# Gate and up products of the feed-forward blocks by Strassen's scheme, with the down product in three groups

## Chip, cores and metric

The kernel runs on one core of one Trainium2 chip. The metric is the device time of one execution in microseconds. In the text, TensorE is PE in the profile, its weight loads are PEld, VectorE is DVE, ScalarE is ACT, GpSimd is POOL and SyncE is SP. A "q" behind an engine's name (SPq, POOLq) means a DMA that this engine issues.

## The reference, cut to what matters

One inference step of a two-layer decoder for 512 prompt tokens and 32 sample tokens, which the kernel handles as one set of T = 544 tokens. Four times (two layers, two blocks each) a feed-forward block stands in it, of width 1024 and inner width 2816:

```python
D_MODEL, D_FF = 1024, 2816

def swiglu(x, w_gu, w_down):
    g, u = jnp.split(x @ w_gu, 2, axis=-1)
    return (jax.nn.silu(g) * u) @ w_down
...
    x = x + 0.5 * swiglu(rmsnorm(x, W['ffn1_norm'][i]), W['ffn1_w_gu'][i], W['ffn1_w_down'][i])
    # token mixer: recurrent block (layer 0) or differential attention (layer 1)
    x = x + 0.5 * swiglu(rmsnorm(x, W['ffn2_norm'][i]), W['ffn2_w_gu'][i], W['ffn2_w_down'][i])
    # a gated per-layer embedding; after layer 0 the shared keys and values are projected
```

Everything is float32 in the reference.

## The kernel before

Activations stand with channels on the 128 partitions and the 544 tokens along the free dimension: `x` is eight tiles (KC = 8) of 128 x 544. A product is worked out in three passes so that it keeps float32's accuracy on 32-bit "fp32r" operands: each operand is cut into a high part (a cast on ScalarE, `act.copy`) and a low part (source minus high part, a subtraction on VectorE), and high times high, high times low and low times high are summed in PSUM. So each block of 128 x 128 weights costs three matmuls for each half of the tokens. `split` (L205) does this for weights, `split_gain` (L217) for activations, with the norm's gain. The norm's other factor, one number per token, is the tile `rb`; it is applied behind the product, since it commutes with it. `mm3` (L188) issues the matmuls: for each input block k, three passes, each in two halves of 256 and 288 tokens.

Weights come in units of at most 128 x 1024 (512 KB). All steps of the program stand in one list, `steps`; the loop at its end keeps the loads (`load_unit`, on SP's queue, into three `raw` tiles) and the splits (`split_unit`, into three pairs `wh` and `wl`) a fixed number of units ahead of the step that runs. A `later` call puts a piece of work off by so many steps. The instructions are then ordered per engine by a scheduler, and every engine takes its own in that order, SP and GpSimd too.

In a feed-forward block (`ffn`), `gate(f)` and `up(f)` alternate for the 22 blocks f of 128 inner channels: one unit each, 48 matmuls each. The gate's result is multiplied by `rb` (L316) and goes through Silu (L317), the up result is multiplied by `rb` (L338) and by the gate's (L339), and the hidden block is split into `hh` (L340) and `hl` (L341), which hold all 22 blocks. Then `down(m, part)` forms eight output blocks m out of three parts of the 22 hidden blocks each (8, 7 and 7, the table `DOWN`), all three in one PSUM accumulation; L352 adds half of it to `x`, and `x_ready` makes the next stage's operands and the sum of squares for its norm. PSUM has four tiles of 128 x 1024 in turn (`new_ps`).

At the start, `x` and the first two weight units arrive in pieces in between, and gate and up of f = 0 run as the pieces come. Before the second block of layer 1, `x` can only be split into `xgh` and `xgl` once attention's output product has read them (`o_done`).

## Time and profile before

| quantity | value |
| --- | --- |
| device time, three runs | 2251.68, 2255.66 and 2256.83 us; median 2255.66 us |
| the profiled execution | 2249.68 us |
| its span, first to last instruction | 2247.8 us |
| mean granted TensorE clock | 0.992 of full speed |
| PE busy, PEld busy | 2194.9 us, 2139.6 us |
| DVE busy, ACT busy, POOL busy | 1069.4 us, 787.3 us, 187.7 us |
| matmuls | 17029 |

The profiled execution has 1.9 us outside its span and lies 6.0 us (0.27%) under the median of the three runs. Matmuls are pipelined, so a matmul's own duration in a row is longer than its share of the time; the spacing of matmuls is read from a stretch of time and the number of them in it.

### The profile page before, as it was taken

To read this page: it belongs to the slowest core of one execution; us is meant where nothing else is said; L and a number is where in the kernel's file an instruction comes from. 1 tells how busy PE (TensorE), PEld (TensorE's weight loads), DVE (VectorE), ACT (ScalarE), POOL (GpSimd) and SP (SyncE) were. 2 spreads that over 40 slices of the span, in tenths; PEclk is the share of its full clock that TensorE was granted. 3 is DMA by queue.
4 is the path that set the end of the run, shared out by engine and by line. 5 is a ranking of instruction groups with operands and counts; after the bars stand their busy time and mean duration, and the time that the engine had idled before them with its cause. 6 is when DMAs were issued, how large, how long until landed. Compare 5 with 4: busy or idle time off the path is not lost.

```text
span 2247.8 us, 39360 instructions
## 1 busy us (share of the span) xinstructions
PE 2194.9 (98%) x17029; PEld 2139.6 (95%) x17029; DVE 1069.4 (48%) x1661; ACT 787.3 (35%) x1132; POOL 187.7 (8%) x219
## 2 busy tenths in 40 slices
PE   9999999999999999999999999999879999999997
PEld 9999999999999999999899999999646999999997
DVE  7444423676544442357444444226656544443255
ACT  4222222596322222244232222223654422222243
POOL 0000001121000000011000000012430200000003
PEclk9999999999999999999999999999989999999998
DMA  4222233255222223233742322347992322223331
GB/s 160 92 85 88 87 88 88 96 125 132 85 87 93 85 87 90 81 100 114 230 154 85 94 86 82 111 129 214 243 279 63 113 86 90 89 84 86 90 108 51
DMA packets 87901, 248.89 MB, mean 111 GB/s; under 512 B 11120, under 2 KB 23168, under 8 KB 87600
## 3 DMA queue, kind: packets, MB, share of 16 engines
q1 hardware_dynamic: 78640, 217.13, 32.0%
q0 software_dynamic: 8400, 28.66, 4.8%
q8 instruction: 133, 2.18, 0.4%
q10 hardware_dynamic: 688, 0.60, 0.1%
q14 instruction: 40, 0.33, 0.1%
HBM read 216.18 MB, written 17.58 MB: 104 GB/s over the span
## 4 chain that ended last, share of the span: by engine, by line
PE 90%; ACT 2%; DMA 2%; DVE 2%; issue 1%; POOL 1%; another core or an unknown queue 0%; SPq 0%; DVEq 0%; POOLq 0%; ACTq 0%
PE ps L197 82%; PE ps L760 2%; PE g L197 1%; DMA raw<-in_wq 1%; PE s L197 1%; DMA vt<-vscr 0%; PE o L1162 0%; DMA xgh<-in_cache_k,idx 0%; PE ss L1178 0%; DMA x<-in_cache_v,idx 0%; PE S L989 0%; PE s L1109 0%; DMA x<-in_x 0%; ACT L447 0%
## 5 line engine op out<-in xcount | busy, mean ns | idle before, releaser
L206 ACT CAST wh<-raw 128x1024 fp32r<-128x1024 f32 (+2 forms) x334 | 336.1, 1007 | 1165.9 <-PE ps L197 1033.5
L197 PE MATMUL ps<-xgh,wl 128*128 128x256 f32 (+1 forms) x3360 | 697.0, 288 | 2.1 <-DMA wl<-raw 2.1
L197 PE MATMUL ps<-xgh,wh 128*128 128x256 f32 (+1 forms) x3360 | 695.9, 289 | 2.5 <-DVE x L1293 1.1
L197 PE MATMUL ps<-xgl,wh 128*128 128x256 f32 (+1 forms) x3360 | 694.3, 288 | 0.1
L197 PEld LDWEIGHTS ps<-xgh,wh 128*128 128x128 f32 x3360 | 543.5, 189 | 4.3 <-DVE x L1293 1.3
L197 PEld LDWEIGHTS ps<-xgl,wh 128*128 128x128 f32 x3360 | 541.6, 189 | 0.3 <-DVE xgl L219 0.3
L197 PEld LDWEIGHTS ps<-xgh,wl 128*128 128x128 f32 x3360 | 538.3, 188 | 2.5 <-DMA wl<-raw 2.5
L207 DVE TENSOR_TENSOR wl<-raw,wh 128x1024 fp32r<-128x1024 f32 (+2 forms) x334 | 389.4, 1166 | 289.9 <-ACT wh L206 285.3
L197 PE MATMUL ps<-hh,wl 128*128 128x256 f32 (+1 forms) x1408 | 290.9, 288 | 0.0
L197 PE MATMUL ps<-hh,wh 128*128 128x256 f32 (+1 forms) x1408 | 290.5, 287 | 0.0
L197 PE MATMUL ps<-hl,wh 128*128 128x256 f32 (+1 forms) x1408 | 288.3, 286 | 0.0
L197 PEld LDWEIGHTS ps<-hl,wh 128*128 128x128 f32 x1408 | 225.7, 188 | 0.0
L197 PEld LDWEIGHTS ps<-hh,wh 128*128 128x128 f32 x1408 | 225.0, 188 | 0.0
L197 PEld LDWEIGHTS ps<-hh,wl 128*128 128x128 f32 x1408 | 224.3, 188 | 0.0
L338 DVE TENSOR_TENSOR t<-ps,rb 128x544 f32<-128x544 f32 x88 | 63.7, 724 | 325.8 <-PE ps L197 325.8
L265 POOL TENSOR_TENSOR acc<-acc,sq 128x544 f32<-128x544 f32 x42 | 68.0, 1620 | 1671.1 <-ACT sq L264 1671.0
L316 DVE TENSOR_TENSOR t<-ps,rb 128x544 f32<-128x544 f32 x88 | 63.8, 724 | 213.5 <-PE ps L197 213.5
L340 ACT CAST hh<-t 128x544 fp32r<-128x544 f32 x88 | 57.0, 648 | 73.3 <-DVE t L339 73.3
L352 DVE SCALAR_TENSOR_TENSOR x<-ps,x 128x544 f32<-128x544 f32 x32 | 23.2, 725 | 109.8 <-PE ps L197 109.8
L339 DVE TENSOR_TENSOR t<-t,t 128x544 f32<-128x544 f32 x88 | 63.8, 725 | 10.0 <-ACT t L317 1.5
L341 DVE TENSOR_TENSOR hl<-t,hh 128x544 fp32r<-128x544 f32 x88 | 63.3, 719 | 5.1 <-ACT hh L340 5.1
L317 ACT ACTIVATE t<-t 128x544 f32<-128x544 f32 x88 | 58.0, 660 | 7.3 <-DVE t L316 6.7
(369 smaller groups left out, 2094.2 us busy)
## 6 DMA issues: line engine op xcount, KB each, us to landing
raw<-in_ffn_gu SPq DMA_DIRECT2D x174, 512.0 KB
raw<-in_ffn_dn SPq DMA_DIRECT2D x64, 448.0 KB
raw<-in_ffn_dn SPq DMA_DIRECT2D x32, 512.0 KB
raw<-in_rg_in SPq DMA_DIRECT2D x16, 512.0 KB
raw<-in_ple_gate SPq DMA_DIRECT2D x16, 512.0 KB
kst<-kscr SPq DMA_DIRECT2D x16, 512.0 KB
wl<-raw POOLq DMA_DIRECT2D x15, 512.0 KB, 4.7
raw<-in_rg_out SPq DMA_DIRECT2D x8, 512.0 KB
```

What stands on the lines that cost most here:

```text
L197: pe.matmul(ps[:, p0:p1], w[:, wc * P : (wc + 1) * P], a[:, k, t0:t1], start=first and q == 0 and s == 0, stop=last and q == n - 1 and s == 2,
L206: first = act.copy(hi, src)
L207: eng.tensor_tensor(lo, src, hi.bitcast(F32), op=OP.subtract)
L265: (eng or (dve if m == KC - 1 else pool)).tensor_tensor(norm["acc"], norm["acc"], sq, op=OP.add)
L316: dve.tensor_tensor(t1, body(ps), norm["rb"], op=OP.mult)
L317: act.activation(t1, t1, AF.Silu)
L338: dve.tensor_tensor(t2, body(ps), norm["rb"], op=OP.mult)
L339: dve.tensor_tensor(t2, t2, t1, op=OP.mult)
L340: act.copy(box["hh"][:, f, :], t2)
L341: later(lambda: dve.tensor_tensor(box["hl"][:, f, :], t2, box["hh"][:, f, :].bitcast(F32), op=OP.subtract))
L352: dve.scalar_tensor_tensor(x[:, m, :], body(ps), 0.5, x[:, m, :], op0=OP.mult, op1=OP.add)
L760: pe.matmul(banks[c], a[:, k, t0:t1], w[:, wv], start=k == 0 and s == 0, stop=k == KC - 1 and s == 2)
```

## The change

The gate's and the up product's weights for one f are seen as a matrix of two by two blocks: the first and second half of the 1024 input channels (four blocks of 128 each), times gate and up. The tokens are cut into two halves of TH = 272. Two outputs (gate, up) for two halves of tokens out of two halves of channels are eight block products; Strassen's scheme (in Winograd's form) forms them from seven products of sums and differences, each 4 x 3 matmuls of 128 x 272.

The activations' sums and differences are formed once per block of the program (`operand_main`, `operand_more`; the new pair of tiles `e`). The weights' sums are formed for every f. Of seven weight operands of 128 x 512, three are stored weights (the unit x, with two of them, and the tile `a`), two are formed by a load followed by an accumulating DMA from GpSimd's queue into the tile `r` (two buffers), and two by additions on VectorE (`sum6`, `sum3`), which need `r` and x. So each f has three units: x, y (first half of `r`) and z (second half of `r`), and `a`, which `low4` splits on its own into the single-buffered `w4h`, `w4l`. The seven products run as steps s0 to s6, with two of them (s1, s4) one f behind: s0(f), s1(f-1), s2(f), s3(f), s4(f-1), s5(f), s6(f). Products 7, 4, 6 and 3 go on in a PSUM area in which an earlier product's partial sum has just been copied out (L453, L468, L501) or read (L460, L479). `first_cycle` does f = 0, product by product interleaved over k.

`rb` is applied to the gate only; the up result stays without it, and the down product gets it instead (`down_done`). The 22 hidden blocks are formed in the three groups of `DOWN`: after 8 (7, 7) of them come all eight down products of this group, each added to `x`. `hh` and `hl` hold eight blocks, used again by each group.

```diff
@@ -287,82 +301,313 @@
...
+    def operand_main(m, gain):
+        xm = x[:, m, :]
+        if m < KC // 2:
+            u = (F.get("w") or F["tmp"]).tile([P, T], F32, tag="t2", name="u", bufs=2 if F.get("w") else 1)
+            act.copy(u[:, :TH], xm[:, :TH])
+            dve.tensor_tensor(u[:, TH:], xm[:, :TH], xm[:, TH:], op=OP.subtract)
+            xm = u
...
+    def operand_more(m, gain):
+        k = m - KC // 2
+        pp = F.get("w") or F["tmp"]
+        bk = pp.tile([P, T], F32, tag="t1", name="bk")
+        bm = pp.tile([P, T], F32, tag="t1", name="bm")
+        e = pp.tile([P, 3, TH], F32, tag="cc", name="e", bufs=2 if F.get("w") else 1)
+        act.activation(bk, x[:, k, :], AF.Copy, scale=v(gain, k))
+        act.activation(bm, x[:, m, :], AF.Copy, scale=v(gain, m))
+        dve.tensor_tensor(e[:, 0], bm[:, TH:], bk[:, TH:], op=OP.subtract)
+        dve.scalar_tensor_tensor(e[:, 1], e[:, 0], -1.0, bk[:, :TH], op0=OP.mult, op1=OP.subtract)
+        dve.scalar_tensor_tensor(e[:, 2], e[:, 1], -1.0, bm[:, :TH], op0=OP.mult, op1=OP.subtract)
+        split(F["e"][0][:, k], F["e"][1][:, k], e)
...
+    def second(q, k):
+        if q in (1, 5):
+            return [t.parts[0][:, k, TH * (q == 5) : TH * (q == 5) + TH] for t in (xgh, xgl)]
+        if q in (2, 3):
+            return [t.parts[1][:, k, TH * (q == 3) : TH * (q == 3) + TH] for t in (xgh, xgl)]
+        return [t[:, k, {7: 0, 6: 1, 4: 2}[q], :] for t in F["e"]]
...
+    def product(ps, q, w, c0, ks=range(KC // 2), first=True):
+        wh, wl = w
+        for k in ks:
+            bh, bl = second(q, k)
+            for s, (a, b) in enumerate(((wh, bh), (wh, bl), (wl, bh))):
+                pe.matmul(
+                    ps, a[:, c0 + k * P : c0 + k * P + P], b,
+                    start=first and k == 0 and s == 0, stop=k == KC // 2 - 1 and s == 2, skip_group_check=True,
+                )
...
+        def late_low(hi, lo, src):
+            act.copy(hi, src)
+            later(lambda: dve.tensor_tensor(lo, src, hi.bitcast(F32), op=OP.subtract))
...
+        def unit_y(f):
+            src = wgu[l, f]
+            u = U[f]
+            def load():
+                r = u["r"] = F["w"].tile([P, 4, 512], F32, tag="r", name="r")
+                sp.dma_start(r[:, 0:4:2, :], src[:, 1:3, :])
+                pool.dma_start(r[:, 0:4:2, :], src[:, 0:2, :], accum_op=OP.add)
+                u["a"] = F["w"].tile([P, 512], F32, tag="a", name="a")
+                sp.dma_start(u["a"], src[:, 0, :])
+            def cut():
+                sum6(f)
+                hi, lo = pair()
+                late_low(hi, lo, u["r"][:, 0:2, :].rearrange("p k n -> p (k n)"))
+                return hi, lo
+            return {"load": load, "split": cut, "open": lambda: F.get("w") is not None}
...
+        def unit_z(f):
+            u = U[f]
+            def cut():
+                sum3(f)
+                hi, lo = pair()
+                late_low(hi, lo, u["r"][:, 2:4, :].rearrange("p k n -> p (k n)"))
+                return hi, lo
+            return {"load": lambda: None, "split": cut, "open": lambda: True}
+        def sum6(f):
+            u = U[f]
+            if "s6" not in u:
+                u["s6"] = dve.tensor_tensor(u["r"][:, 1, :], u["r"][:, 0, :], u["x"][:, :512], op=OP.add)
+        def sum3(f):
+            u = U[f]
+            if "s3" not in u:
+                u["s3"] = dve.tensor_tensor(u["r"][:, 3, :], u["r"][:, 1, :], u["x"][:, 512:], op=OP.add)
...
+        def low4(f):
+            u = U[f]
+            u["w4"] = [F["w"].tile([P, 512], F32R, tag=n, name=n, bufs=1) for n in ("w4h", "w4l")]
+            late_low(*u["w4"], u["a"])
...
+        def begin(f):
+            u = U[f]
+            u["ps"] = new_ps()
+            u["b"], u["a_"] = u["ps"][:, :TH], u["ps"][:, 512 : 512 + TH]
+            u["cc"] = F["w"].tile([P, 3, TH], F32, tag="cc", name="cc")
+        def s0(f):
+            u = U[f]
+            begin(f)
+            product(u["b"], 1, ready[u["ix"]], 0)
+            act.copy(u["cc"][:, 0], u["b"])
+        def s1(f):
+            u = U[f]
+            product(u["b"], 7, ready[u["iz"]], 0, first=False)
+            t1 = u["t1"] = F["w"].tile([P, T], F32, tag="t1", name="t1")
+            dve.tensor_tensor(t1[:, TH:], u["b"], u["cc"][:, 2], op=OP.add)
+            dve.tensor_tensor(t1[:, TH:], t1[:, TH:], norm["rb"][:, TH:], op=OP.mult)
+            finish()
...
+        def s2(f):
+            u = U[f]
+            u["c"] = new_ps()[:, :TH]
+            product(u["c"], 5, ready[u["iy"]], 0)
+            act.copy(u["cc"][:, 2], u["c"])
...
+        def s3(f):
+            u = U[f]
+            product(u["a_"], 2, ready[u["ix"]], 512)
+            up_first(f)
+            finish()
...
+        def s4(f):
+            u = U[f]
+            product(u["b"], 4, u["w4"], 0, first=False)
+            t1 = u["t1"]
+            dve.tensor_tensor(t1[:, :TH], u["b"], norm["rb"][:, :TH], op=OP.mult)
+            act.activation(t1, t1, AF.Silu, scale=-1.0)
+            def hidden():
+                t2, q = u["t2"], f - H["a"]
+                dve.tensor_tensor(t2, t2, t1, op=OP.mult)
+                act.copy(H["hh"][:, q, :], t2)
+                later(lambda: dve.tensor_tensor(H["hl"][:, q, :], t2, H["hh"][:, q, :].bitcast(F32), op=OP.subtract), 3 if f < H["b"] - 1 else 1)
+            later(hidden, 2 if f < H["b"] - 1 else 1)
+        def s5(f):
+            u = U[f]
+            if f + 1 < H["b"]:
+                sum6(f + 1)
+            product(u["b"], 6, ready[u["iy"]], 512, first=False)
+            act.copy(u["cc"][:, 1], u["b"])
+            finish()
+        def s6(f):
+            u = U[f]
+            product(u["c"], 3, ready[u["iz"]], 512, first=False)
+            dve.tensor_tensor(u["t2"][:, TH:], u["c"], u["cc"][:, 1], op=OP.add)
+            low4(f)
...
+        def first_cycle(f):
+            u = U[f]
+            begin(f)
+            u["c"] = new_ps()[:, :TH]
+            for k in range(KC // 2):
+                product(u["b"], 1, ready[u["ix"]], 0, [k])
+                product(u["c"], 5, ready[u["iy"]], 0, [k])
+            act.copy(u["cc"][:, 0], u["b"])
+            act.copy(u["cc"][:, 2], u["c"])
+            for k in range(KC // 2):
+                product(u["a_"], 2, ready[u["ix"]], 512, [k])
+                product(u["c"], 3, ready[u["iz"]], 512, [k], first=False)
+                product(u["b"], 6, ready[u["iy"]], 512, [k], first=False)
+            up_first(f)
+            finish()
+            act.copy(u["cc"][:, 1], u["b"])
+            finish()
+            dve.tensor_tensor(u["t2"][:, TH:], u["c"], u["cc"][:, 1], op=OP.add)
+            low4(f)
+            norm_done()
...
+        def down_done(m, part):
+            ps = H.pop(("ps", m))
+            t = F["w"].tile([P, T], F32, tag="t1", name="dn")
+            dve.scalar_tensor_tensor(t, body(ps), 0.5, norm["rb"], op0=OP.mult, op1=OP.mult)
+            dve.tensor_tensor(x[:, m, :], x[:, m, :], t, op=OP.add)
+            if part == len(DOWN) - 1:
...
+        def step(fn, *args):
+            add(None, lambda: fn(*args), -1)
+        for part, (a, b) in enumerate(DOWN):
+            for f in range(a, b):
+                u = U[f]
+                u["ix"], u["iy"], u["iz"] = (add_unit(q(f)) for q in (unit_x, unit_y, unit_z))
+                if f == a:
+                    add(None, lambda a=a, b=b: group(a, b))
+                if f == 0:
+                    step(first_cycle, 0)
+                    continue
+                step(s0, f)
+                if f > a:
+                    step(s1, f - 1)
+                step(s2, f)
+                step(s3, f)
...
+                    step(s4, f - 1)
+                step(s5, f)
+                step(s6, f)
+            step(s1, b - 1)
+            add(wdn[l, 0][:, a:b, :], down(0, part))
+            step(s4, b - 1)
+            step(down_rest, part)
+            for m in range(1, KC):
                 add(wdn[l, m][:, a:b, :], down(m, part))
...
         def o_done(m, ps):
...
             if m == KC - 1:
                 for k in range(KC):
-                    split_gain(xgh[:, k, :], xgl[:, k, :], x[:, k, :], v(gain_out, k))
+                    operand_main(k, gain_out)
+            if m >= KC // 2:
+                operand_more(m, gain_out)
...
+    def may_load():
+        if at["dma"] >= n:
+            return False
+        u = units[at["dma"]]
+        if isinstance(u, dict):
+            return at["dma"] < at["split"] + 6 and u["open"]()
+        return at["dma"] < at["split"] + 3
+    def pump(hold):
+        while at["split"] < min(n, at["done"] + 3 - max(hold, 0)):
+            while at["dma"] <= at["split"]:
+                load_unit()
+            split_unit()
+        while may_load():
+            load_unit()
...
+    def quarters(w):
+        r = w.reshape(2, 2, KC // 2, P, 2, FC, P).transpose(0, 5, 3, 4, 1, 2, 6)
+        return np.ascontiguousarray(np.stack([r[:, :, :, 0, 1], r[:, :, :, 0, 0], r[:, :, :, 1, 0], r[:, :, :, 1, 1]], 3)).reshape(2, FC, P, 4, 512)
```

Also changed: pools move so that the tiles `e`, `r`, `a` and the new temporaries fit, `tables()` is issued after the fifth down product of the first group, and the loads of units x, y, z may run up to six units ahead of the splits.

The order in which VectorE takes its work in a feed-forward block, before, for one f. Names are those of the code, with a number for each allocation (`ps`: a PSUM tile; `hl_198`: the low hidden part):

```order
L316 TENSOR_TENSOR t1_945<-ps_896,rb_367 128x544
L207 TENSOR_TENSOR wl_949<-raw_775,wh_948 128x1024
L338 TENSOR_TENSOR t2_1003<-ps_954,rb_367 128x544
L339 TENSOR_TENSOR t2_1003<-t2_1003,t1_945 128x544
L207 TENSOR_TENSOR wl_1008<-raw_834,wh_1007 128x1024
L341 TENSOR_TENSOR hl_198<-t2_1003,hh_197 128x544
```

These are four passes over 544 tokens and two weight splits.

And now, for one f in the middle of a group, from the last row of the f ahead. `r_2035` and `raw_2001` are the tile `r` and the unit x of f + 1, `r_1912` is the tile `r` of f itself, with the rows between in the order of their steps:

```order
L492 TENSOR_TENSOR hl_247<-t2_1996,hh_246 128x544
L427 TENSOR_TENSOR r_2035<-r_2035,raw_2001 128x512
L432 TENSOR_TENSOR r_2035<-r_2035,raw_2001 128x512
L460 TENSOR_TENSOR t1_2213<-ps_2060,cc_2061 128x272
L461 TENSOR_TENSOR t1_2213<-t1_2213,rb_348 128x272
L371 TENSOR_TENSOR wl_2218<-r_1912,wh_2217 128x1024
L479 TENSOR_TENSOR t2_2248<-ps_2186,cc_2187 128x272
L371 TENSOR_TENSOR wl_2251<-raw_2001,wh_2250 128x1024
L485 TENSOR_TENSOR t1_2213<-ps_2060,rb_348 128x272
L371 TENSOR_TENSOR w4l_2309<-a_1915,w4h_2308 128x512
L490 TENSOR_TENSOR t2_2122<-t2_2122,t1_2213 128x544
L371 TENSOR_TENSOR wl_2285<-r_2035,wh_2284 128x1024
```

VectorE's two sums in the newly arrived `r_2035` now stand ahead of the partial gate (L460, L461) and ahead of the last use of the other buffer, `r_1912` (the row `wl_2218`). SP's queue in the same place:

```order
L382 DMA raw_2127<-in_ffn1_gu 128x1024
L403 DMA a_1915<-in_ffn1_gu 128x512
L400 DMA r_2035<-in_ffn1_gu 128x2x512
L382 DMA raw_2253<-in_ffn1_gu 128x1024
L403 DMA a_2038<-in_ffn1_gu 128x512
L400 DMA r_2161<-in_ffn1_gu 128x2x512
```

The load into a buffer `r` is followed on GpSimd's queue by its accumulation, `r_1912`, `r_2035`, `r_2161` in turn, one after each load. `r_2161` takes the buffer of `r_1912`, so its load waits for the row `wl_2218` above; the sums of `r_2161` then stand one cycle later in VectorE's queue, again ahead of the row that frees `r_2035`.

At the program's start VectorE's queue now holds these rows (`e`, `el`: the new activation operand; `acc`: sum of squares; `r_254` and `r_261`: the `r` of f = 1 and f = 2; `wl_371`: the unit x of f = 1):

```order
L221 TENSOR_TENSOR el_103<-e_193,eh_102 128x816
L334 TENSOR_TENSOR e_209<-bm_208,bk_207 128x272
L279 TENSOR_TENSOR acc_217<-acc_217,sq_237 128x544
L335 SCALAR_TENSOR_TENSOR e_209<-e_209,bk_207 128x272
L371 TENSOR_TENSOR w4l_337<-a_118,w4h_336 128x512
L336 SCALAR_TENSOR_TENSOR e_209<-e_209,bm_208 128x272
L221 TENSOR_TENSOR accl_340<-acc_217,acch_339 128x544
L432 TENSOR_TENSOR r_254<-r_254,raw_252 128x512
L221 TENSOR_TENSOR el_103<-e_209,eh_102 128x816
L427 TENSOR_TENSOR r_261<-r_261,raw_259 128x512
L432 TENSOR_TENSOR r_261<-r_261,raw_259 128x512
L479 TENSOR_TENSOR t2_332<-ps_267,cc_268 128x272
```

They stand behind 39 others, among them eight splits of `x` and three of weights. The sums for f = 2 (`r_261`, in the buffer that f = 0 frees) stand ahead of the split of f = 1's own unit x.

## Rows read from the trace of the kernel before

**Rows 1.** Page: busy time by engine, chain by engine, chain by line.

```profile
PE 2194.9 (98%) x17029; PEld 2139.6 (95%) x17029; DVE 1069.4 (48%) x1661; ACT 787.3 (35%) x1132; POOL 187.7 (8%) x219
PE 90%; ACT 2%; DMA 2%; DVE 2%; issue 1%; POOL 1%; another core or an unknown queue 0%; SPq 0%; DVEq 0%; POOLq 0%; ACTq 0%
PE ps L197 82%; PE ps L760 2%; PE g L197 1%; DMA raw<-in_wq 1%; PE s L197 1%; DMA vt<-vscr 0%; PE o L1162 0%; DMA xgh<-in_cache_k,idx 0%; PE ss L1178 0%; DMA x<-in_cache_v,idx 0%; PE S L989 0%; PE s L1109 0%; DMA x<-in_x 0%; ACT L447 0%
```

**Rows 2.** Windows by stage: gate/up, down, key projection, second layer's second gate/up start, program start.

```profile
core 0: us, PE busy (x) PEld busy (x) DVE busy (x) ACT busy (x) POOL busy (x), PEclk, DMA share, GB/s
50.00:230.00 180.00, 180.00 (x1436) 180.00 (x1435) 79.47 (x103) 50.70 (x61) 0.00 (x0) 1.00 0.28 89
275.00:406.00 131.00, 131.00 (x1053) 131.00 (x1052) 39.44 (x41) 33.19 (x39) 9.53 (x6) 1.00 0.31 89
1038.00:1082.00 44.00, 43.90 (x350) 43.82 (x351) 31.08 (x55) 12.08 (x15) 3.13 (x6) 1.00 0.50 152
1742.00:1779.00 37.00, 37.00 (x295) 37.00 (x296) 17.71 (x21) 18.44 (x25) 11.49 (x8) 1.00 0.46 128
0.00:30.00 30.00, 27.38 (x190) 26.50 (x191) 20.58 (x35) 18.50 (x27) 2.66 (x9) 1.00 0.69 226
```

**Rows 3.** Timeline of VectorE, 150 to 158 us: start, duration, operation, idle before it.

```profile
154.52 0.73 DVE L338 TENSOR_TENSOR t<-ps,rb 128x544 f32<-128x544 f32 x1 [3.92 <-PE ps L197]
155.35 0.73 DVE L339 TENSOR_TENSOR t<-t,t 128x544 f32<-128x544 f32 x1
155.99 1.22 DVE L207 TENSOR_TENSOR wl<-raw,wh 128x1024 fp32r<-128x1024 f32 x1
157.12 0.72 DVE L341 TENSOR_TENSOR hl<-t,hh 128x544 fp32r<-128x544 f32 x1
```

**Rows 4.** Groups by form: ScalarE casts and Silu.

```profile
L206 ACT CAST wh<-raw 128x1024 fp32r<-128x1024 f32 x256 | 269.2, 1052 | 875.6 <-PE ps L197 744.8 <-issue 104.1 <-PE ps L760 12.6
L317 ACT ACTIVATE t<-t 128x544 f32<-128x544 f32 x88 | 58.0, 660 | 7.3 <-DVE t L316 6.7 <-DVE e_g L1396 0.5
```

**Rows 5.** A weight load: VectorE row, load's issue, windows of the transfer.

```profile
599.15 1.22 DVE L207 TENSOR_TENSOR wl<-raw,wh 128x1024 fp32r<-128x1024 f32 x1
...
600.40 0.33 SPq L168 DMA_DIRECT2D raw<-in_ffn_gu  x1
...
600.50:601.00 0.50, 0.50 (x7) 0.50 (x6) 0.50 (x1) 0.00 (x0) 0.00 (x0) 1.00 0.00 0
601.00:601.50 0.50, 0.50 (x7) 0.50 (x6) 0.00 (x1) 0.00 (x0) 0.00 (x0) 1.00 0.75 66
603.00:603.50 0.50, 0.50 (x6) 0.50 (x5) 0.00 (x0) 0.01 (x1) 0.00 (x0) 1.00 0.55 221
603.50:604.00 0.50, 0.50 (x6) 0.50 (x5) 0.30 (x1) 0.50 (x1) 0.00 (x0) 1.00 0.00 0
```

**Rows 6.** Timelines of SP and ScalarE: loads of in_wv, and the cast that waits.

```profile
1087.01 0.92 SPq L168 DMA_DIRECT2D raw<-in_wv  x2
...
1091.11 1.05 ACT L206 CAST wh<-raw 128x1024 fp32r<-128x1024 f32 x1 [4.27 <-DMA raw<-in_wv]
```

**Rows 7.** Accumulating transfer: ScalarE row, GpSimd's issue, page's landing times.

```profile
480.09 1.04 ACT L213 ACTIVATE wl<-wh 128x1024 fp32r<-128x1024 f32 x1
...
481.43 0.85 POOL L214 DMA_DIRECT2D wl<-raw  x1 [3.87 <-ACT wl L213]
...
wl<-raw POOLq DMA_DIRECT2D x15, 512.0 KB, 4.7
...
qst<-sph POOLq DMA_DIRECT2D x32, 64.0 KB, 5.7
```

**Rows 8.** Chain in order of time: start and length of pieces.

```profile
9.95 16.36 PE ps L197 x128
27.65 385.09 PE ps L197 x3072
...
1741.92 36.44 PE ps L197 x288
```

More of the change, by code (lines that the diff above doesn't have):

```diff
@@ L141, in trunk_kernel, with add_unit @@
     steps = []
+    units, keeps, raw, ready = [], [], {}, {}
+    def add_unit(unit, keep=None):
+        units.append(unit)
+        keeps.append(keep)
+        return len(units) - 1
     def add(unit, fn, hold=0, keep=None):
+        if unit is not None:
+            add_unit(unit, keep)
         steps.append((unit, fn, hold, keep))
@@ L172, in split_unit @@
     def split_unit():
+        u = units[at["split"]]
+        if isinstance(u, dict):
+            ready[at["split"]] = u["split"]()
+            at["split"] += 1
+            return
         t, cols = raw.pop(at["split"])
@@ L178, in split_unit @@
             lo = wp.tile([P, 1024], F32R, tag="wl", name="wl")
-        with ExitStack() as order:
-            if at["split"] == 5:
-                order.enter_context(tc.issue_after(norm["read"].ins))
-            done_by[at["split"]] = (split_adding if at["split"] in slow else split)(h[:, :cols], lo[:, :cols], t[:, :cols])
+        done_by[at["split"]] = (split_adding if at["split"] in slow else split)(h[:, :cols], lo[:, :cols], t[:, :cols])
         ready[at["split"]] = h, lo
@@ new lines, in operand @@
+    def operand(m, gain, pp=None):
+        F["tmp"] = pp
+        operand_main(m, gain)
+        if m >= KC // 2:
+            operand_more(m, gain)
+    def second(q, k):
[13 more added lines that the diff above has]
+                )
@@ new lines, in go, with down_rest, group @@
+                down_part(m, part, range(a, b), w, True, True)
+                down_done(m, part)
+                if beside and part == 0 and m == 4:
+                    beside()
+            return go
+        def down_rest(part):
+            a, b = DOWN[part]
+            down_part(0, part, range(a + 4, b - 1), H["w0"], False, False)
+        def group(a, b):
+            H["a"], H["b"] = a, b
+            if a == 0:
+                hp, H["close"] = open_pool("ffnh", bufs=1, side="right")
+                H["hh"] = hp.tile([P, KC, T], F32R, name="hh")
+                H["hl"] = hp.tile([P, KC, T], F32R, name="hl")
@@ L524, in out_step @@
             return go
-        base = len([u for u, _, _, _ in steps if u is not None]) + 2 * KC
+        base = len(units) + 2 * KC
         slow.update(range(base - 8, base + 2))
@@ L1272, in early_more @@
                 mm3(*A["w", m], [(k, k) for k in range(4, 7)], xgh, xgl, first=False, last=False)
-        base = len([u for u, _, _, _ in steps if u is not None]) + KC
+        base = len(units) + KC
         slow.update(range(base + 0, base + 6))
@@ L1431, in trunk_kernel @@
     add(None, start)
-    ffn(0, "ffn1", "mix0", late=True)
-    steps.insert(6, (None, begin_tables, 0, None))
+    ffn(0, "ffn1", "mix0", beside=begin_tables)
     recurrent("ffn20")
@@ L1441, in trunk_kernel @@
     ple_final(1)
[L1444 to L1445 removed]
     n = len(units)
+    def may_load():
+        if at["dma"] >= n:
+            return False
+        u = units[at["dma"]]
+        if isinstance(u, dict):
+            return at["dma"] < at["split"] + 6 and u["open"]()
[4 more added lines that the diff above has]
+                load_unit()
+            split_unit()
+        while may_load():
+            load_unit()
     for u, fn, hold, _ in steps:
```

211 lines of the change are left out of this document (110 added, 101 removed).

## The prediction

> **What bounds the kernel now.** First the page: TensorE is busy for 2194.9 us, 98% of the span, with weight loads beside it for 2139.6 us, and in the chain of work that ended last it has 90%, of which the matmuls of `mm3` (L197) alone are 82% [rows 1]. No other engine reaches half. Then the windows by stage: in 50 to 230 us (gate and up) TensorE never idles and issues 1436 matmuls in 180 us, so one costs 125.3 ns; VectorE is busy for 79.47 us of the 180, ScalarE for 50.70, the DMA engines for 28% [rows 2]. The down products look the same (1053 matmuls in 131 us, VectorE 39.44). So fewer gate and up matmuls is time saved, one for one, as long as the others deliver; the question is what becomes late.
>
> **Matmuls removed.** Per f there were 2 units x 48 = 96 matmuls, now 7 x 12 = 84. The mean width was (256 + 288)/2 = 272 and stays 272, so I keep 125.3 ns. Over 22 x 4 = 88 f that is 88 x 12 x 0.1253 = **-132.3 us**; a cycle of one f falls from 12.03 to 10.53 us. Down matmuls stay as many.
>
> **What VectorE, ScalarE and the DMA have per f.** VectorE's rows start 0.64 us apart at 544 columns (155.35 to 155.99) and 1.13 us apart at 1024 (155.99 to 157.12); a row that needs the one ahead of it adds 0.19 (154.52 to 155.35 is 0.83) [rows 3]. That is 1.02 ns a column and 0.085 us an instruction: 0.61 at 512, 0.36 at 272. Per f it now has three splits of 1024 (3.39), a split and two sums of 512 (1.83), five rows of 272 (1.80) and two of 544 (1.28), 8.3 us, and with two or three dependent pairs 8.7 of the 10.53; it had 79.47/180 x 12.03 = 5.3 of 12.03. ScalarE: three casts at 1.052 us and a Silu at 0.66 [rows 4], and by width half a cast (0.53), three copies of 272 (about 0.35 each) and a cast of 544 (0.65): 6.1 us. DMA: 0.28 of 12.03 us for 1 MB before is 3.4 us; now 1.75 MB, with 0.5 MB of sums read back and written once more 2.25 MB, is at most 7.6. None passes 10.53, so in a steady cycle TensorE stays the bound, if every operand arrives in turn.
>
> **The ring of two `r`.** This is what may not. A new `r` is loaded when the z split of the f two ahead has read its buffer; the load lands, GpSimd issues the accumulation, it lands, and only then can VectorE take the two sums. In its queue these stand, as the order shows, ahead of the partial gate of f (L460, L461) and of f's z split, which frees the other buffer and so starts the next such trip. One trip is thus a cycle of its own, and if it takes longer than 10.53 us TensorE waits: product 4 goes on in the PSUM area that L460 reads, and L460 is queued behind the sums.
>
> The legs of a trip. (a) SP wakes in about 0.05 us (600.37 to 600.40), and the transfer's data end in the slice 603.00 to 603.50, some 3.1 us after the split that freed the buffer [rows 5]; a queue in which ScalarE waits for a load gives 4.1 (1087.01 to 1091.11) [rows 6]. Both carry 512 KB, as here. I take the middle, 3.6. (b) GpSimd issues 0.3 us after what it waits for (481.13 to 481.43), and an accumulation of 512 KB lands 4.7 us after its issue [rows 7]; one of 64 KB, in another stage, needs 5.7. I take 4.7. With a wake on either side that makes L = 8.7 us; the bounds are 8.2 (3.1 us) and 10.2 (4.1 and 5.7). (c) VectorE: the two sums, dependent (0.80 + 0.61), L460 (0.55, behind them), L461 (0.36) and the z split (1.22, to its end): 3.5 us. A trip is 12.2 us and the excess over a cycle e = 1.67 us (1.17 to 3.17).
>
> It does not bind in every f. At each group's start two `r` have been fetched beside the down products, which use none, and the group's first cycle has only five products. Of a group's seven or eight cycles I count four as bound, and 0.3 us of slack left over. There are 12 groups (three in each of four blocks): 12 x (4 x 1.67 - 0.3) = **+76.6 us**; at the bounds 53 and 148. It is hidden altogether if L is 7.0 or less.
>
> **The program's start.** Before, the chain has 128 matmuls in the 16.36 us from 9.95, and from 27.65 us they run without a gap for 385 us [rows 8]. Of the 190 matmuls in the first 30 us [rows 2], 18 fall behind 27.65, 24 only warm the engine up and 4 are the norm's: 144 products' matmuls are done by then. Now f = 0 has 60 matmuls, and f = 1 cannot begin until VectorE has split its unit x. VectorE stands ahead of it with four subtractions and eight splits of x, twelve rows and four 816-wide splits for `e`, weight splits, sums and squares, about 28 us by the column price, from the 5th microsecond: 34. Next in its queue are the sums for f = 2, whose buffer f = 0's z split frees at about 27; with L that is 36, then sums and split: product 1 of f = 1 at 39. TensorE is then behind by (39 - 27.65)/0.1253 + 144 - 60 = 175 matmuls, **+22 us**. Before, VectorE has 20.58 us of work in these 30, so it covers its part [rows 2]; a start bound by loads alone would be some 4 us less, a late `e` 4 more.
>
> **Other transitions.** The second block of layer 1 makes all its operands when attention's output product ends: four chains of `e` (three rows and a split each) and the late splits of `x` are some 9.5 us of VectorE, against 7.5 us of a first cycle (60 x 0.1253); before, 288 matmuls followed in 36.44 us without a stall [rows 8], and VectorE had 17.71 us in 37 [rows 2]. +3. Behind the key projection VectorE has 31.08 of 44 us and gets 9.6 more, which still fits, tightly: +2. **Sum +5** (0 to 10).
>
> **Costed at nothing.** Each down product now ends in two VectorE rows per group where one per block stood (192 for 32, 0.64 to 0.83 us each): their cover is the 5.3 to 6.0 us of a step's 42 to 48 matmuls, of which VectorE used a third (39.44 of 131); uncovered they would be 160 x 0.7 = 112 us. The tail of a group (product 4, gate, Silu, product, cast, low part) takes some 3.6 us and the last hidden block is wanted by `down_rest`; the first down product's matmuls over the other blocks, 6 us, lie between. Without them it would be 12 x 3.6 = 43.
>
> **Sum.** -132.3 + 22 + 5 + 76.6 = -28.7 against the profiled execution's 2249.7: 2221. The median of the runs lies 6.0 us above that execution, so **2227 us**.
>
> **Rivals.** *The ring is hidden.* If the transfers, with little else on the queues, need L of 7.0 or less, nothing of the 76.6 is left: 2249.7 - 132.3 + 27 + 6 = 2150. The 3.1 us row and a DMA share of 0.28 speak for it, the 4.7 us accumulation against: 3.1 + 4.7 + 0.4 is already 8.2. (By the Trainium skill, "DMA: Bandwidth & Descriptors", section "Anatomy of one DMA — SWDGE (gpsimd) path", a transfer takes 2.0 us plus its bytes over 436 KB per us, by estimate 3.2 us for 512 KB and 6.4 for both legs, which would give this case; the load's row agrees, the accumulation's 4.7 does not, and the measurement decides.) Chance 0.17.
>
> *The ring is slower* and takes back everything. The gain left without it is 105 us; it is used up at e = 2.27 us, which is L = 9.3, only 0.6 above my value. With 4.1 us for the load and 5.7 for the accumulation (L = 10.2): 12 x (4 x 3.17 - 0.3) = 148, so 2249.7 - 105.3 + 148 + 6 = 2299, slower than before. For it speak that three transfers and an accumulation per f now share queues that had two loads; against it that the 5.7 us row is of another kind of transfer. Also, were six instead of four cycles of a group bound, L = 8.4 would do. Chance 0.18.
>
> *VectorE becomes the bound.* By full durations (1.22, 0.73) its rows sum to 9.4 us per f; with 0.19 for every wait on another engine it would come to about 11.5, one over the cycle, 88 us in the ring's place: 2249.7 - 105.3 + 88 + 6 = 2238 us. Its dense rows, 1.13 after each other, speak against. It decides from 10.53 us. Chance 0.07.
>
> **How the numbers follow.** My forecast, ring partly binding, has 0.58, with a range of its own of 2204 to 2265 (L from 8.2 to 9.5, the start's 4 us either way). A measurement of this kernel tells about 0.2%, 4.5 us, from no change. Faster: 0.17 + 0.48 of the 0.58 + 0.05 of VectorE's = 0.70. Same: 0.05, L near 9.3. Slower: 0.18 + the rest = 0.25. The range for 8 in 10 has to take in most of both outer cases: 2150 to 2292.
>
> **What would show it.** Matmuls 125 ns apart inside a product, 84 per f. TensorE idle ahead of product 4 (L359, with `w4h`), released by VectorE's L460; VectorE idle ahead of L427, released by a DMA into `r`; GpSimd's accumulation (L401) landing 4.7 us after issue; cycles of 10.5 us at a group's start and about 12.2 later in it. VectorE's busy time rises from 1069 us to about 1,500. The first product of f = 1 at about 39 us. I am wrong if cycles are 10.5 throughout (ring hidden), if VectorE shows no idle time in them (VectorE bound), or if TensorE waits at a group's end or in `down`, which I costed at nothing.

## The result and the profile after

The changed kernel takes 2446.23 us in the median (2441.05 to 2453.01, four runs), the kernel before 2256.24 us beside it: a ratio of 1.0845, 95% interval 1.0808 to 1.0881. It is slower by 8.5%, where 1.3% faster was forecast and the range ended at 2292.

The page of the profiled execution (2453.01 us, span 2451.2): busy time of TensorE and VectorE, the chain that ended last by engine and by line, and the landing times of the gate and up loads.

```profile
PE 2183.6 (89%) x15973; PEld 2097.4 (86%) x15973; DVE 1537.3 (63%) x2516; ACT 1056.9 (43%) x1635; POOL 292.8 (12%) x307
...
PE 46%; DMA 30%; DVE 15%; issue 5%; ACT 3%; POOL 0%; SPq 0%; POOLq 0%; DVEq 0%; ACTq 0%
PE ps L211 29%; DMA r<-in_ffn_gu 25%; PE ps L359 11%; DVE wl L371 3%; DVE r L427 2%; DVE r L432 2%; PE ps L1020 1%; PE g L211 1%; DVE t L460 1%; DMA x<-in_cache_v,idx 1%; DVE t L461 1%; DMA wl<-raw 1%; DVE wl L221 1%; DVE xgl L233 1%; DMA v
...
r<-in_ffn_gu SPq DMA_DIRECT2D x88, 512.0 KB, 3.8
r<-in_ffn_gu POOLq DMA_DIRECT2D x88, 512.0 KB, 6.8
raw<-in_ffn_gu SPq DMA_DIRECT2D x87, 512.0 KB, 4.1
...
a<-in_ffn_gu SPq DMA_DIRECT2D x88, 256.0 KB, 4.5
```

Against [rows 1]: the 1056 matmuls are gone as planned (17029 to 15973), but TensorE is busy for almost as long, and in the chain its share fell from 90% to 46%. DMA has 30% now, 25 of them transfers into `r`. VectorE is busy for 63% of the span, so it is not what bounds the kernel as a whole.

The windows of the same kernel: the first group's gate and up after its start, and the down products behind it.

```profile
core 0: us, PE busy (x) PEld busy (x) DVE busy (x) ACT busy (x) POOL busy (x), PEclk, DMA share, GB/s
50.00:144.00 94.00, 80.74 (x565) 79.13 (x564) 65.35 (x152) 40.34 (x61) 8.37 (x7) 0.89 0.53 131
148.80:194.00 45.20, 45.20 (x362) 45.20 (x361) 22.63 (x29) 9.28 (x11) 0.00 (x0) 1.00 0.28 89
```

Beside [rows 2]: gate and up issue 565 matmuls in 94 us, one per 166 ns, and TensorE idles for 13 of them. The down products still keep it full, 362 in 45.2 us. So the loss in this group sits in gate and up.

One cycle of these, from the timeline of the same kernel (SP, GpSimd, VectorE and TensorE by time; in brackets the idle time before a row and what ended it):

```profile
67.43 0.38 SPq L400 DMA_DIRECT2D r<-in_ffn_gu  x1
70.46 0.33 SPq L382 DMA_DIRECT2D raw<-in_ffn_gu  x1
71.41 0.33 SPq L403 DMA_DIRECT2D a<-in_ffn_gu  x1
71.74 1.20 POOL L401 DMA_DIRECT2D r<-in_ffn_gu  x1 [15.34 <-DVE e_i L1665]
...
79.85 0.69 DVE L427 TENSOR_TENSOR r<-r,raw 128x512 f32<-128x512 f32 x1 [4.33 <-DMA r<-in_ffn_gu]
80.58 0.69 DVE L432 TENSOR_TENSOR r<-r,raw 128x512 f32<-128x512 f32 x1
81.19 0.43 DVE L460 TENSOR_TENSOR t<-ps,cc 128x272 f32<-128x272 f32 x1
81.66 0.44 DVE L461 TENSOR_TENSOR t<-t,rb 128x272 f32<-128x272 f32 x1
81.68 0.48 PE L359 MATMUL ps<-eh,w4h 128*128 128x272 f32 x1 [2.22 <-DVE t L460]
82.01 1.22 DVE L371 TENSOR_TENSOR wl<-r,wh 128x1024 fp32r<-128x1024 f32 x1
...
83.26 0.38 SPq L400 DMA_DIRECT2D r<-in_ffn_gu  x1
```

This is the trip of the prediction, leg by leg. SP loads `r` at 67.43; GpSimd issues the accumulation at 71.74; it lands at about 79.83, 8.1 us later; VectorE, idle for 4.33 us, takes the two sums, then the partial gate that product 4 waited for, then the z split, and that frees the buffer for the load at 83.26. The trip is 15.8 us long; 12.2 was forecast. (The bracket of the row at 71.74 names a VectorE row that had ended 0.2 us before; summed over the span, the largest part of GpSimd's waits ahead of L401 is put down to the load into `r`, 778.5 us, as the next view shows.)

From start to start of product 4, 64 cycles of full length can be read in this trace (the last of a group has six products and is left out). Their mean is 14.14 us, and 51 of them are over 12.5. The waits of TensorE, GpSimd and VectorE, summed over the span (total in us, number, longest):

```profile
PE ps L359 <- DVE t L460: 154.1, 59, 4.5
PE ps L359 <- DVE t L479: 13.6, 30, 4.6
PE outp L1314 <- DMA x<-in_cache_v,idx: 11.8, 3, 5.9
...
POOL r L401 <- DMA r<-in_ffn_gu: 778.5, 58, 24.9
DVE r L427 <- DMA r<-in_ffn_gu: 254.6, 57, 6.4
```

154.1 us in 59 waits stand ahead of product 4, released by L460, as the prediction named it, and VectorE waits for 254.6 us ahead of L427 for transfers into `r`.

### The profile page after: what moved, and what is told of

Same layout as the page of the kernel before. It is cut to its first block, busy times and chain, and to the rows that moved or that the text cites. A ratio compares the mean times of both kernels' runs of the same rounds, so it can differ in the third digit from the quotient of the medians.

```text
span 2451.2 us, 39182 instructions
## 1 busy us (share of the span) xinstructions
PE 2183.6 (89%) x15973; PEld 2097.4 (86%) x15973; DVE 1537.3 (63%) x2516; ACT 1056.9 (43%) x1635; POOL 292.8 (12%) x307
## 4 chain that ended last, share of the span: by engine, by line
PE 46%; DMA 30%; DVE 15%; issue 5%; ACT 3%; POOL 0%; SPq 0%; POOLq 0%; DVEq 0%; ACTq 0%
PE ps L211 29%; DMA r<-in_ffn_gu 25%; PE ps L359 11%; DVE wl L371 3%; DVE r L427 2%; DVE r L432 2%; PE ps L1020 1%; PE g L211 1%; DVE t L460 1%; DMA x<-in_cache_v,idx 1%; DVE t L461 1%; DMA wl<-raw 1%; DVE wl L221 1%; DVE xgl L233 1%; DMA vt<-vscr 1%
## 5 line engine op out<-in xcount | busy, mean ns | idle before, releaser
L359 PE MATMUL ps<-xgh,wh 128*128 128x272 f32 x1408 | 414.9, 295 | 21.1 <-ACT cc L518 10.3
L359 PE MATMUL ps<-xgl,wh 128*128 128x272 f32 x1408 | 412.7, 293 | 5.7 <-DVE xgl L233 5.6
L359 PE MATMUL ps<-xgh,wl 128*128 128x272 f32 x1408 | 413.1, 293 | 4.5 <-DVE wl L371 4.3
L359 PEld LDWEIGHTS ps<-xgh,wh 128*128 128x128 f32 x1408 | 272.1, 193 | 23.7 <-ACT wh L370 11.2
L427 DVE TENSOR_TENSOR r<-r,raw 128x512 f32<-128x512 f32 x88 | 62.0, 705 | 355.2 <-DMA r<-in_ffn_gu 254.6
L401 POOL DMA_DIRECT2D r<-in_ffn_gu x88 | 106.4, 1209 | 1459.9 <-DMA r<-in_ffn_gu 778.5
L359 PEld LDWEIGHTS ps<-xgl,wh 128*128 128x128 f32 x1408 | 272.0, 193 | 7.1 <-DVE xgl L233 7.1
L359 PEld LDWEIGHTS ps<-xgh,wl 128*128 128x128 f32 x1408 | 271.4, 193 | 5.9 <-DVE wl L371 5.5
L371 DVE TENSOR_TENSOR wl<-r,wh 128x1024 fp32r<-128x1024 f32 x176 | 214.8, 1221 | 71.2 <-ACT wh L370 70.0
L359 PE MATMUL ps<-eh,w4h 128*128 128x272 f32 x352 | 121.7, 346 | 154.2 <-DVE t L460 154.1
L359 PE MATMUL ps<-eh,wh 128*128 128x272 f32 x704 | 223.4, 317 | 18.4 <-DVE t L479 13.6
L359 PE MATMUL ps<-el,wh 128*128 128x272 f32 x704 | 216.3, 307 | 0.0
L359 PE MATMUL ps<-eh,wl 128*128 128x272 f32 x704 | 215.2, 306 | 0.0
```

The costliest lines, as they stand in the source:

```text
L359: pe.matmul(ps, a[:, c0 + k * P : c0 + k * P + P], b, start=first and k == 0 and s == 0, stop=k == KC // 2 - 1 and s == 2, skip_group_chec ...
L371: later(lambda: dve.tensor_tensor(lo, src, hi.bitcast(F32), op=OP.subtract))
L401: pool.dma_start(r[:, 0:4:2, :], src[:, 0:2, :], accum_op=OP.add)
L427: u["s6"] = dve.tensor_tensor(u["r"][:, 1, :], u["r"][:, 0, :], u["x"][:, :512], op=OP.add)
```

## Experiments

**The sums later in VectorE's queue.** The work is unchanged; an ordering edge puts the first sum of f + 1 behind the low part of f + 1's own unit x (the row `xl`, remembered where it is issued); the second sum reads the first and follows it.

```diff
...
             if "s6" not in u:
                 u["s6"] = dve.tensor_tensor(u["r"][:, 1, :], u["r"][:, 0, :], u["x"][:, :512], op=OP.add)
+                if "xl" in u:
+                    tc.add_manual_dep(u["s6"].ins, u["xl"].ins.name, NOSYNC, reason="sums behind the split of x")
```

> Same work, another order on VectorE: the two sums of f + 1 stand behind the low part of f + 1's unit x, and so behind the partial gate and the z split of f. Ring theory: the sums then wait for nothing, the z split that frees a buffer no longer stands behind an accumulation, and the 64 steady cycles, which are 14.7 us in the middle of a group and 231 us too long together, fall to about 10.5; with some 3 us less at each group's start the time is near 2190 us (2160 to 2230). Rival, transfers too slow in any order: a trip of 12.3 us still meets its sums late, cycles stay above 12 us and the time above 2300. Rival, VectorE is the bound by its own work: VectorE shows no idle time, cycles of 12 us, about 2300.

Measured: 2189.47 us (2185.27 to 2193.66), ratio to the kernel before 0.9707 (0.969 to 0.9723). The cycles are 10.58 us in the mean and none is over 12.5. Its page:

```profile
PE 2088.7 (96%) x15973; PEld 2025.1 (93%) x15973; DVE 1538.2 (70%) x2516; ACT 1058.9 (48%) x1635; POOL 293.9 (13%) x307
...
PE 81%; DVE 6%; DMA 6%; ACT 4%; issue 2%; POOL 1%; SPq 0%; DVEq 0%; ACTq 0%; POOLq 0%
...
r<-in_ffn_gu POOLq DMA_DIRECT2D x88, 512.0 KB, 8.0
```

Two of its windows, the first group's gate and up, and the whole first block from its start on, group ends and down products included (columns as above):

```profile
46.00:113.60 67.60, 67.60 (x539) 67.60 (x538) 62.60 (x151) 38.27 (x58) 7.17 (x6) 1.00 0.70 170
46.00:399.00 353.00, 353.00 (x2806) 352.60 (x2805) 255.78 (x419) 158.29 (x227) 32.19 (x27) 1.00 0.54 136
```

And one trip in its timeline:

```profile
68.00 0.38 SPq L405 DMA_DIRECT2D r<-in_ffn_gu  x1
...
73.62 1.20 POOL L406 DMA_DIRECT2D r<-in_ffn_gu  x1 [9.69 <-DVE t L497]
...
77.53 1.17 DVE L373 TENSOR_TENSOR wl<-r,wh 128x1024 fp32r<-128x1024 f32 x1
...
78.73 0.38 SPq L405 DMA_DIRECT2D r<-in_ffn_gu  x1
...
82.05 0.68 DVE L432 TENSOR_TENSOR r<-r,raw 128x512 f32<-128x512 f32 x1
...
83.89 0.68 DVE L439 TENSOR_TENSOR r<-r,raw 128x512 f32<-128x512 f32 x1
```

The accumulation is no faster, 8.0 us against 6.8. But the other buffer is freed at 78.7, before the sums of the `r` loaded at 68.00 (82.05, without idle time ahead of them), so the next load no longer waits for this accumulation. TensorE never idles in the first window, 125.4 ns per matmul, though VectorE is busy for 62.60 of 67.60 us. (The margin is thin: in the next trip the sums wait 0.75 us for their transfer, at 93.12, but no full cycle is over 10.7 us.) The place of the two sums alone cost 2446.2 - 2189.5 = 257 us, and the rival of a VectorE at its limit falls.

**Without the accumulations.**

```diff
-                pool.dma_start(r[:, 0:4:2, :], src[:, 0:2, :], accum_op=OP.add)
```

> Leaves out the 88 accumulating transfers (the second summand of two weight operands is missing), all else as in the changed kernel. Ring theory: the trip falls from about 15 us to 3.7 + 3.5, below a cycle, so the ring is hidden: cycles of 10.5, time near 2190 us (2160 to 2230). Rival, VectorE's or ScalarE's work is the bound: cycles stay at 12 or more, above 2300. If this is much faster than the kernel with the late sums, the accumulations cost something besides their latency in the ring.

Measured: 2178.96 us, ratio 0.9658 (0.9633 to 0.9683); cycles of 10.58. A short trip hides the ring in the old order too, and what is left of the accumulations in the kernel with the late sums is 10.5 us. This run also has 512 KB less to move per f, but the late sums move all of it and are fast, so the load on the DMA engines is not the cause. Order and latency are thus two halves of one cause: changing either far enough removes it.

**The accumulation with the DMA engines to itself.**

The loads of a(f) and of the next unit x get an edge with a wait (`acc` is the accumulation).

```diff
...
-                sp.dma_start(u["x"], src[:, 2:4, :].rearrange("p k n -> p (k n)"))
+                ins = sp.dma_start(u["x"], src[:, 2:4, :].rearrange("p k n -> p (k n)"))
+                if f > 3:
+                    tc.add_manual_dep(ins.ins, U[f - 1]["acc"].ins.name, BEHIND, reason="behind the accumulation")
...
-                sp.dma_start(u["a"], src[:, 0, :])
+                ins = sp.dma_start(u["a"], src[:, 0, :])
+                if f > 3:
+                    tc.add_manual_dep(ins.ins, u["acc"].ins.name, BEHIND, reason="behind the accumulation")
```

> Same work; the loads of a(f) and of the next unit x wait until the accumulation of f has landed, so that it has the DMA engines to itself. If sharing with these loads is what makes an accumulation take 6.8 us in place of 4.7: it lands in about 4.7, L is 9, cycles of 12.5, time near 2330 us (2290 to 2370). If it is slow by itself (8 us alone): no change, 2446, or slower by the loads that come later.

Measured: 2424.19 us, ratio 1.073 (1.0707 to 1.0752); cycles of 13.99. Its page:

```profile
r<-in_ffn_gu SPq DMA_DIRECT2D x88, 512.0 KB, 4.0
r<-in_ffn_gu POOLq DMA_DIRECT2D x88, 512.0 KB, 6.7
```

Over the 88 of them the accumulation still needs 6.7 us. Sharing explains a small part: the median of the three accumulations between 60 and 110 us falls from 8.0 to 6.8, and the kernel is 22 us faster, but 4.7 is not reached. The first reading missed.

**One piece of 4 KB in place of two of 2 KB.**

```diff
-                pool.dma_start(r[:, 0:4:2, :], src[:, 0:2, :], accum_op=OP.add)
+                pool.dma_start(r[:, 0:2, :], src[:, 0:2, :], accum_op=OP.add)
...
```

The plain load ahead of it, the sums and the splits follow the new layout.

> Same work, another layout of r: the two blocks that are loaded and accumulated lie next to each other, so a partition's part of the transfer is one piece of 4 KB on both sides in place of two of 2 KB; VectorE's order as in the changed kernel. If the pieces make the accumulation slow (6.8 us median against the 4.7 us of the row that the prediction took, which had 4 KB pieces): it lands in about 4.7, steady cycles of 14.7 fall to about 12.5, time near 2320 us. If it is slow because its source is in HBM and not in SBUF as in that row: no change, 2446 within 20.

Measured: 2449.21 us, ratio 1.086 (1.0839 to 1.0882); cycles of 14.11, accumulations of 7.1 us. The pieces are not it.

**The second summand from SBUF.**

```diff
-                pool.dma_start(r[:, 0:4:2, :], src[:, 0:2, :], accum_op=OP.add)
+                s = F["w"].tile([P, 2, 512], F32, tag="s", name="s", bufs=1)
+                sp.dma_start(s, src[:, 0:2, :])
+                pool.dma_start(r[:, 0:4:2, :], s, accum_op=OP.add)
```

> Same work; the second summand is first loaded into a tile of its own beside the first, and the accumulation goes from SBUF to SBUF, in pieces of 2 KB. If the source in HBM makes it slow: it lands in about 4.7 us, the load leg grows from 3.8 to about 4.8 (two loads of 512 KB at once), cycles of about 13.5, time near 2380 us. If not: the load leg's growth alone is added, cycles of 15.7, about 2500 us.

Measured: 2369.99 us, ratio 1.0503 (1.0483 to 1.0524); cycles of 12.92. Its page:

```profile
r<-in_ffn_gu SPq DMA_DIRECT2D x88, 512.0 KB, 3.9
s<-in_ffn_gu SPq DMA_DIRECT2D x88, 512.0 KB, 3.8
r<-s POOLq DMA_DIRECT2D x88, 512.0 KB, 5.5
```

With 512 KB more to move per f, the kernel is 76 us faster; the accumulation falls to 5.5 us, and the load into `r` stays at 3.9, where 4.8 was expected. So the source is a part of it: from HBM 6.8, from SBUF 5.5, and 4.7 in the row of before [rows 7], whose source is the SBUF tile `raw`. Why 5.5 and not 4.7 was not tried.

**The groups alone.** The kernel before, its eight products untouched, with the loop over groups.

```diff
...
-        for f in range(FC):
-            add(wgu[l, f], gate(f))
-            add(wgu[l, FC + f], up(f))
-        for m in range(KC):
-            for part, (a, b) in enumerate(DOWN):
+        for part, (a, b) in enumerate(DOWN):
+            for f in range(a, b):
+                add(wgu[l, f], gate(f))
+                add(wgu[l, FC + f], up(f))
+            for m in range(KC):
                 add(wdn[l, m][:, a:b, :], down(m, part))
```

> The kernel before with the second part of the change alone: eight-product gate and up as before, but the down products of a group of 8, 7 and 7 hidden blocks right behind that group, each added to x. The prediction costed the groups at nothing: 2256 us within 6. Rival, groups cost something at each of their 12 ends or by their 64 more VectorE rows of 0.8 us: up to 12 x 3.6 + some = 2300 us.

Measured: 2258.91 us, ratio 1.0007 (0.9994 to 1.002). In the kernel before, costing them at nothing was right, to 3 us or so. This version has one VectorE row per down product where the changed kernel has two; there the window 46 to 399 us of the late sums says the same, since TensorE is busy for all 353 us of it, group ends and down products included.

**The sums at a third place**, directly behind the z split of f: the edge of the first experiment, to that row.

> Same work, the sums of f + 1 at a third place in VectorE's queue: directly behind the z split of f, three rows (some 3 us) ahead of where the late sums stand. They no longer hold back a split that frees a buffer, but with the late sums a trip's transfers need 4.7 + 0.3 + 8.0 = 13.1 us after the z split, and this place comes a cycle, 10.6 us, behind it. So VectorE stalls there by 13.1 less the cycle, beside 8.7 us of work: a cycle C = 8.7 + 13.1 - C, C = 10.9, some 0.3 us in each of 64 cycles: time near 2189 + 19 = 2208 us. Rival, only whether the sums stand ahead of the freeing split matters: 2189 within 5.

Measured: 2259.17 us, ratio 1.0 (0.9982 to 1.0017); cycles of 11.87. Timeline of VectorE and SP:

```profile
80.89 1.22 DVE L373 TENSOR_TENSOR wl<-r,wh 128x1024 fp32r<-128x1024 f32 x1
82.14 0.38 SPq L405 DMA_DIRECT2D r<-in_ffn_gu  x1
83.02 0.69 DVE L432 TENSOR_TENSOR r<-r,raw 128x512 f32<-128x512 f32 x1 [0.91 <-DMA r<-in_ffn_gu]
...
92.52 1.22 DVE L373 TENSOR_TENSOR wl<-r,wh 128x1024 fp32r<-128x1024 f32 x1
...
94.76 0.69 DVE L432 TENSOR_TENSOR r<-r,raw 128x512 f32<-128x512 f32 x1 [1.02 <-DMA r<-in_ffn_gu]
```

Both readings missed: the place still costs 70 us against the late sums, though the sums no longer stand ahead of the split, and far more than the 19 us expected. VectorE waits for the transfer ahead of the sums (0.91 and 1.02 us), as expected. From the z split's end (82.11) to the sums of that buffer's next contents (94.76) it is 12.65 us. From the sums (83.02) to the next z split's end (93.74) it is 10.72, not the 8.7 us of VectorE's work; over the span its rows also wait for products on the way (61.8 us in 68 waits ahead of L467). TensorE in turn waits for L486, the row behind the sums, for 58.2 us in 49 waits. The two stretches add up to two cycles, 11.6 and 11.7 us here, by the way they are taken; they show where the time goes and are no test of the formula. Three rows of VectorE, some 3 us, decide between a gain of 3% and none.

**The program's start**, on the kernel with the late sums: the products of unit x first, once with and once without moving the additions of squares to GpSimd.

```diff
...
             for k in range(KC // 2):
                 product(u["b"], 1, ready[u["ix"]], 0, [k])
+            act.copy(u["cc"][:, 0], u["b"])
+            for k in range(KC // 2):
+                product(u["a_"], 2, ready[u["ix"]], 512, [k])
+            for k in range(KC // 2):
                 product(u["c"], 5, ready[u["iy"]], 0, [k])
-            act.copy(u["cc"][:, 0], u["b"])
             act.copy(u["cc"][:, 2], u["c"])
             for k in range(KC // 2):
-                product(u["a_"], 2, ready[u["ix"]], 512, [k])
...
         for k in range(KC):
-            square_in(k, pool if k in () else dve)
+            square_in(k, pool)
```

> The kernel with the late sums, and at the program's start the seven additions of squares move from VectorE to GpSimd and the products of f = 0 that need only unit x come ahead of those that need r. If VectorE's list bounds the start: its seven rows of 0.72 us leave the list, product 1 of f = 1, at 40.3 us with the late sums, comes 4 to 5 us sooner, time 2189 - 4 = 2185 us. If the arrival of the accumulated weights bounds it: no change, 2189.

> The kernel with the late sums and, at the program's start, the products of f = 0 that need only unit x ahead of those that need r, but the additions of squares on VectorE again. If VectorE's list bounds the start: no change, 2189 within 4, product 1 of f = 1 at 40 us. If TensorE's idle time there and its halved clock behind it bound it: up to 5 us faster.

Measured with the additions on GpSimd: 2187.84 us, ratio 0.9705 (0.9686 to 0.9723), no gain; f = 1 begins at 45.0 us, later than the 40.3 of the late sums alone. Timeline of GpSimd and VectorE:

```profile
25.48 1.52 POOL L279 TENSOR_TENSOR acc<-acc,sq 128x544 f32<-128x544 f32 x1 [0.77 <-ACT sq L278]
25.72 1.58 DVE L336 SCALAR_TENSOR_TENSOR e<-e,bk 128x272 f32<-128x272 f32 x1
...
27.82 0.43 DVE L337 SCALAR_TENSOR_TENSOR e<-e,bm 128x272 f32<-128x272 f32 x1
...
31.07 1.76 POOL L279 TENSOR_TENSOR acc<-acc,sq 128x544 f32<-128x544 f32 x1 [4.07 <-ACT sq L278]
31.55 1.57 DVE L335 TENSOR_TENSOR e<-bm,bk 128x272 f32<-128x272 f32 x1
```

A row that takes 0.43 us alone takes 1.58 when it begins beside a GpSimd addition, and ends just behind it (25.48 + 1.52 = 27.00; 25.72 + 1.58 = 27.30). In these rows what was taken off VectorE came back as waits on it; that this is why f = 1 begins later was not tried alone.

Measured with the additions on VectorE: 2182.78 us (2181.11 to 2186.84), ratio 0.9667 (0.9649 to 0.9686), the fastest version here, 3.3% under the kernel before. Its profiled execution shows f = 1 at 40.8 us and the same block ends as the late sums, to 2 us, so whether it really is 6.7 us better, as the medians say, stays open: the two were timed on separate occasions.

## Why the prediction was wrong

**Right: the matmuls and the engines.** Where nothing waits, a matmul costs 125.4 ns and a cycle 10.58 us; forecast 125.3 and 10.53. VectorE's work fits the cycle, the groups cost nothing that can be told from zero, and VectorE's busy time (1537 us) was forecast as about 1,500.

**Right: the mechanism that eats the gain.** The traces show the ring, at the place forecast, and the waits at product 4 behind L460. Undoing either side of it, the order or the latency, ends it. The number of bound cycles came out near the one assumed (51 in 12 groups, 48 assumed), but with some luck, for they stand elsewhere: forecast were 10.5 us at a group's start and 12.2 later, while the first group's cycles, from product 4 to product 4, are 14.7, 15.4, 15.6, 14.8, 13.8 and 12.2 us. The `r` fetched ahead bought no free cycle here; the shorter ones come at the end, where no next `r` is waited for.

**Wrong in size: the step (b) of the trip's legs**, "an accumulation of 512 KB lands 4.7 us after its issue [rows 7]". In the first group's cycles it takes 6.1 to 8.7 us, 8.1 in the one above, with L = 12.4 (67.43 to 79.85) for the 8.7 assumed and the upper bound of 10.2; leg (a) is 4.3 us (67.43 to 71.74) with GpSimd's 0.3 in it, for 3.9; leg (c) is 3.4 us (79.85 to 83.23), as forecast. The row of 4.7 was of the same size but with its source in SBUF. The upper bound, 5.7 us from a transfer of 64 KB, was no bound for one of 512 KB from HBM. By the Trainium skill, "DMA: Bandwidth & Descriptors", section "Anatomy of one DMA — SWDGE (gpsimd) path", 2.0 us plus bytes over 436 KB per us makes an estimate of 3.2 us (the section is on transfers from GpSimd's queue, so it bears on this leg and not, as the prediction had it, on SP's load too); no accumulation of 512 KB here comes near it (4.7, 5.5, 6.8), so the rival that it would have borne out lost more clearly than any other.

The 51 cycles that are over 12.5 us have a mean of 14.74. With the excess over 10.53 at 4.2 us, they cost 51 x 4.2 = 214 us, and the whole difference to the late sums, shorter waits included, is 257: 180 us more than the 76.6 forecast. The rival named for this (L = 10.2, 2299 us) had the sign, and a break-even of L = 9.3 that was far exceeded. (Its aside on six bound cycles, L = 8.4, comes to 8.5 by the prediction's own sum.)

**Where the 257 us show up.** 154 of them are idle time ahead of product 4. Most of the rest is in TensorE's busy time: 2183.6 us against 2088.7 with the late sums, for the same 15973 matmuls. Behind about half of the waits the next matmuls run at the lower clock: in the cycle above they start 0.23 us apart from 81.95 on, where 0.125 is the spacing at full clock; the granted clock is 0.89 in that window and 1.00 with the late sums. In a cycle that waits for the ring anyway this only fills what would be idle; that it costs nothing there was argued, not tried.

**The start: near in size, with the same leg too short.** Forecast +22 us. The last down matmul of the first block comes at 399.2 us with the late sums and 406.4 before; without the 33.1 us of a block's saved matmuls (132.3/4) that is +25.9. In the changed kernel f = 1 begins at 39.9 us, forecast 39, but that is in part luck: its first two matmuls need no low part. The split that the forecast had done by 39 stands behind the sums for f = 2, which are ready at 41.45 and not at 36 (loaded at 29.68, so L = 11.8), and the low part is there at 44.4.

**Wrong: the other transitions, +5.** The last down matmuls of the other blocks come at 938.4, 1476.4 and 2107.8 us with the late sums (970.1, 1533.4 and 2169.4 before): in the same way +8.6, +7.8 and +28.5 us, 45 in place of 5. With the ring's 180 these 40 come to about the whole miss, 2446 - 2227 = 219 us. Of the 8.6, 5.1 are one wait at the second block's start, which the sum had put at nothing: in the kernel with the late sums TensorE stands still until ScalarE has copied a partial sum out (L525), a copy that stands in its queue behind the casts for the block's operands.

```profile
572.53 0.60 PE L360 MATMUL ps<-xgh,wh 128*128 128x272 f32 x1 [5.06 <-ACT cc L525]
```

The 7.8 us were not taken apart. The last is attention with the block behind it. Here the 60 matmuls of f = 0 take from 1729.0 to 1749.0 us, 20 in place of 7.5; windows of the kernel with the late sums (columns as above):

```profile
1729.00:1734.00 5.00, 1.67 (x8) 1.25 (x9) 5.00 (x8) 3.64 (x6) 1.50 (x1) 0.94 0.02 3
1734.00:1740.00 6.00, 4.63 (x17) 3.70 (x16) 6.00 (x10) 6.00 (x11) 0.00 (x0) 0.50 0.00 0
1740.00:1745.00 5.00, 3.88 (x17) 3.88 (x18) 4.06 (x8) 2.50 (x5) 0.00 (x0) 0.50 0.27 82
```

The sum had set VectorE's 9.5 us against TensorE's 7.5 at full clock. VectorE needs more: it is busy for 15.1 of these 16 us, with weight splits and squares among its rows that the 9.5 left out, and TensorE waits for them. TensorE also falls to the lower of its two clocks (0.50 granted, 1.2 of 2.4 GHz), at which its matmuls start 0.23 us apart; for the 42 matmuls of these windows that is at most 42 x 0.1 = 4 us, an estimate, and less where it waits anyway. Another 9 us lie in attention itself: from the last down product to its last weight product 206.1 us before, 215.2 with the late sums, with longer waits for the gathered cache (`x<-in_cache_v,idx`: 5.6 us before, 10.7 after) and for `vt<-vscr` (1.3 and 4.9). The groups alone show 6 of these 9 (212.5). The cause was not sought.
